# Two SwiGLU input projections of a streaming-encoder layer computed as 2x2 block products, seven in place of eight, with GpSimd forming the sums of weight blocks

## The chip, the core and the metric

The kernel runs on one core of one Trainium2 chip. The engines named below are PE (TensorE, matrix products), PEld (TensorE loading its stationary operand), ACT (ScalarE), DVE (VectorE), POOL (GpSimd) and SP (SyncE, which here only issues transfers). The metric is the device time of one execution in microseconds (us); lower is better.

## The reference

One layer of a hybrid encoder on 512 prompt tokens and 64 sample tokens, model width 1024, feed-forward width 4096, all in float32. What the change touches is the SwiGLU block, which stands at the start and at the end of the layer:

```python
def swiglu(x, w_in, w_out):
    a, b = jnp.split(x @ w_in, 2, axis=-1)      # w_in 1024 x 8192
    return (jax.nn.silu(a) * b) @ w_out         # w_out 4096 x 1024

x = x + 0.5 * swiglu(rmsnorm(x, norm_ffn1), w_ffn1_in, w_ffn1_out)
x = x + mixer(rmsnorm(x, norm_mix))             # SSD, band attention and mLSTM branches, then w_out
x = x + 0.5 * swiglu(rmsnorm(x, norm_ffn2), w_ffn2_in, w_ffn2_out)
```

A final RMSNorm follows. The mixer's arithmetic is the same in both kernels.

## The kernel before

All 576 tokens run side by side, feature-major: features on the 128 partitions, tokens along the free axis, in two halves of 256 and 320 (`HALVES`). Weights are the stationary operand. Each float32 product is carried by three float32r passes over a high and a low part of both operands (high x high, high x low of the tokens, low of the weights x high), so each tile of 128 input features by 128 output features costs three matmuls for each half of the tokens. One matmul therefore streams 256 or 320 columns, 288 on average.

`weights` (L121) loads the next block of 0.5 MB (`w`, three buffers, issued by SP at L129), casts it to its high part on ACT (`wh`, L132) and subtracts on DVE to get the low part (`wl`, L133). `gemm` (L149) and `matmuls` (L140, the instruction is L146) do the products into one of three PSUM banks (`acc`); with `half_major` a group of blocks is done for one half of the tokens and then for the other. `norm` (L227) writes the token operand, high `XH` on ACT and low `XL` on DVE (`scaled`, L223 and L224, not yet divided by the rms), sums the squares on DVE (`na`, L186) and, through two small PE products (L200, L216), gets `rs`, 1/rms of each token on all partitions.

`ffn` (L308) is the SwiGLU block. `first(i)` makes four tiles of 128 features of the hidden layer: for each one block for a and one for b. The a half is scaled by `rs` on DVE (L322), goes through Silu on ACT (L323) and is scaled again on POOL (L324, `P`); b is multiplied in on DVE (L332, `Q`) and the product is split into `YH` (ACT, L175) and `YL` (DVE, L176). `second(i)` multiplies four such tiles by a row block of w_out: 192 matmuls, 16 evacuations that add to the residual `x` or `R1` (L338). The order is first(0), then first(i), second(i-1) in turn. So one hidden tile of 128 costs 2 blocks x 8 x 3 x 2 = 96 matmuls, and an FFN has 32 of them.

Every instruction goes into its engine's queue in an order that the tile framework's scheduler sets from a simulated timeline; an engine runs its queue in that order, waiting on semaphores. Tiles share buffers by tag, and a tile that reuses a buffer waits until its last reader is done.

```python
def weights(self, desc):                                                    # L121
    w = self.wp.tile([128, 1024], F32, name="w", tag="w", bufs=3)
    nc.sync.dma_start(w, self.I["wblk"][i])                                 # L129
    nc.scalar.copy(hi, w)                                                   # L132
    nc.vector.tensor_tensor(lo, w, hi.bitcast(F32), op=ALU.subtract)        # L133
def matmuls(self, ps, h, hi, lo, c0, step, nk, xh, xl, k0):                 # L140
    for k in range(nk):
        for i, (wt, xx) in enumerate(((hi, xh), (hi, xl), (lo, xh))):
            nc.tensor.matmul(ps[:, :n], wt[:, wsl], xx[:, k0 + k, a:a + n], ...)   # L146
```

Of the kernel before, what the change touches and what calls it, by code (L numbers as in the profile page):

```python
# [15 lines left out]
F32 = mybir.dt.float32  # L16
# [9 lines left out]
NB = 293  # L26
# [3 lines left out]
# the parts of the mixer: attention (pairs of heads), mLSTM (heads), SSD (groups); the recurrences' gates  # L30
# are worked out after number GATES of them
# [4 lines left out]
# columns of the packed per-feature constants  # L36
# [11 lines left out]
# columns of w_in  # L48
# [6 lines left out]
class Hybrid:  # L55
    def __init__(self, ctx, tc, I, O):
        self.tc, self.nc, self.I, self.O = tc, tc.nc, I, O
        self.plan = []
        self.ahead = {}
# [18 lines left out]
    # Slots of a tag are given out in program order, so tiles share a tag only if they are first  # L78
    # written in that order.
# [15 lines left out]
    def setup(self):  # L95
# [13 lines left out]
        # 1 where column >= partition  # L109
# [11 lines left out]
    def weights(self, desc):  # L121
        """The next block of 0.5 MB: its high and low parts."""
# [26 lines left out]
    def gemm(self, tiles, xh, xl, k0=0, half_major=False, order=(0, 1)):  # L149
        """tiles: (desc, [(c0, evac), ...]); desc = (name, row0, rows, col0, cols)."""  # L150
# [27 lines left out]
    def sumsq(self, x, k, h, acc):  # L178
# [5 lines left out]
        sq = self.wp.tile([128, 320], F32, name="sq", tag="sq", bufs=3)  # L184
# [3 lines left out]
    def rsqrt(self, r, src, m, scale):  # L188
        """r[:, :m] = (scale * src + eps) ** -0.5, a few columns."""
# [818 lines left out]
```

## Time and profile before

| what | value |
|---|---|
| time, median of 3 runs | 2066.32 us (2065.57 to 2066.57) |
| span of the profiled execution, first to last instruction | 2064.8 us |
| PE busy | 2046.7 us, 99% |
| DVE / ACT / POOL busy | 1022.9 / 659.1 / 342.5 us |
| weight blocks loaded | 293 of 0.5 MB |
| clock granted to PE, mean | 0.996 |

A profiled execution has no time of its own in the results beside its span; the span lies 1.5 us under the median. Tables of instructions give the line, engine, operation, output and inputs by name, shape, count, busy time, mean duration in ns of one, and the idle time before. A matmul's duration is longer than the distance between two starts, since they are pipelined: the pace is read from starts or from counts in a window.

### The profile page before, as it was taken

How to read it: one execution, taken by the hardware profiler on the slowest of the kernel's cores; microseconds unless marked ns; L12 is line 12 of the kernel's file. 1: busy time of each engine (PE TensorE's matmuls, PEld its weight loads, DVE VectorE, ACT ScalarE, POOL GpSimd, SP SyncE). 2: the span in 40 equal slices, each digit the busy share in tenths (PEclk: the TensorE clock that was granted, in tenths of full speed). 3: DMA queues.
4: the chain of work that ended last, by engine and by line, in shares of the span. 5: the costliest groups of instructions: out<-in, count | busy, mean ns of one | idle time of the engine just before them, and what ended most of it. 6: DMA issues, size and time to landing. Idle time of an engine off the chain costs nothing. (4 is left out here: it accounts for less than half of the span.)

```text
span 2064.8 us, 36478 instructions
## 1 busy us (share of the span) xinstructions
PE 2046.7 (99%) x15269; PEld 1999.4 (97%) x15269; DVE 1022.9 (50%) x1956; ACT 659.1 (32%) x1174; POOL 342.5 (17%) x448
## 2 busy tenths in 40 slices
PE   8999999999999999999999999999999999999998
PEld 7999999999999888989999999999999999999998
DVE  6344444444446856466777535345444444444445
ACT  3222222222224345454445223234322222222223
POOL 4101101101100010202443201320111011011011
PEclk9999999999999999999999999999999999999999
DMA  3222222222224322322333222222222222222221
GB/s 140 85 86 85 84 83 82 82 82 83 82 93 150 109 87 70 101 65 72 114 104 105 70 82 108 103 81 82 82 82 83 83 86 85 85 83 82 82 82 57
DMA packets 63131, 182.90 MB, mean 89 GB/s; under 512 B 6752, under 2 KB 18656, under 8 KB 62840
## 3 DMA queue, kind: packets, MB, share of 16 engines
q1 hardware_dynamic: 61992, 179.44, 24.9%
q8 instruction: 120, 1.97, 0.4%
q10 hardware_dynamic: 976, 1.14, 0.2%
q14 instruction: 43, 0.35, 0.1%
HBM read 171.80 MB, written 8.76 MB: 87 GB/s over the span
## 5 line engine op out<-in xcount | busy, mean ns | idle before, releaser
L146 PE MATMUL acc<-XH,wh 128*128 128x256 f32 (+1 forms) x3408 | 1014.3, 298 | 5.1 <-DVE P L322 4.7
L146 PE MATMUL acc<-XL,wh 128*128 128x256 f32 (+1 forms) x3408 | 1012.7, 297 | 2.3 <-DVE XL L224 2.2
L146 PE MATMUL acc<-XH,wl 128*128 128x256 f32 (+1 forms) x3408 | 1014.4, 298 | 0.0
L146 PEld LDWEIGHTS acc<-XL,wh 128*128 128x128 f32 x3408 | 645.2, 189 | 9.3 <-issue 5.4
L146 PEld LDWEIGHTS acc<-XH,wh 128*128 128x128 f32 x3408 | 642.0, 188 | 12.0 <-DVE P L322 5.1
L146 PEld LDWEIGHTS acc<-XH,wl 128*128 128x128 f32 x3408 | 640.9, 188 | 5.1 <-issue 4.7
L132 ACT CAST wh<-w 128x1024 fp32r<-128x1024 f32 x293 | 307.3, 1049 | 829.6 <-PE acc L146 720.0
L133 DVE TENSOR_TENSOR wl<-w,wh 128x1024 fp32r<-128x1024 f32 x293 | 364.9, 1245 | 124.0 <-ACT wh L132 123.3
L146 PE MATMUL acc<-YH,wl 128*128 128x320 f32 (+1 forms) x1280 | 378.6, 296 | 0.0
L146 PE MATMUL acc<-YH,wh 128*128 128x320 f32 (+1 forms) x1280 | 378.4, 296 | 0.0
L146 PE MATMUL acc<-YL,wh 128*128 128x320 f32 (+1 forms) x1280 | 376.9, 294 | 0.0
L324 POOL TENSOR_TENSOR P<-P,rs 128x320 f32<-128x320 f32 (+1 forms) x128 | 145.8, 1140 | 961.8 <-ACT P L323 961.8
L146 PEld LDWEIGHTS acc<-YL,wh 128*128 128x128 f32 x1280 | 241.9, 189 | 0.0
L146 PEld LDWEIGHTS acc<-YH,wh 128*128 128x128 f32 x1280 | 240.4, 188 | 0.2 <-issue 0.2
L146 PEld LDWEIGHTS acc<-YH,wl 128*128 128x128 f32 x1280 | 239.9, 187 | 0.1
L322 DVE TENSOR_TENSOR P<-acc,rs 128x320 f32<-128x320 f32 (+1 forms) x128 | 58.5, 458 | 215.2 <-PE acc L146 212.9
L332 DVE TENSOR_TENSOR Q<-acc,P 128x256 f32<-128x256 f32 (+1 forms) x128 | 58.7, 459 | 184.2 <-PE acc L146 139.1
L338 DVE SCALAR_TENSOR_TENSOR R<-acc,R 128x256 f32<-128x256 f32 (+1 forms) x128 | 58.5, 457 | 84.6 <-PE acc L146 84.3
L323 ACT ACTIVATE P<-P 128x320 f32<-128x320 f32 (+1 forms) x128 | 56.4, 442 | 137.0 <-DVE P L322 137.0
L338 DVE SCALAR_TENSOR_TENSOR x<-acc,x 128x256 f32<-128x256 f32 (+1 forms) x128 | 58.4, 456 | 81.9 <-PE acc L146 81.7
L175 ACT CAST YH<-Q 128x256 fp32r<-128x256 f32 (+1 forms) x128 | 55.1, 430 | 131.5 <-DVE Q L332 131.5
L176 DVE TENSOR_TENSOR YL<-Q,YH 128x256 fp32r<-128x256 f32 (+1 forms) x128 | 58.2, 455 | 30.3 <-ACT YH L175 30.3
(274 smaller groups left out, 1230.9 us busy)
## 6 DMA issues: line engine op xcount, KB each, us to landing
w<-in_wblk SPq DMA_DIRECT2D x293, 512.0 KB, 3.4
b<-scr_rows SPq DMA_DIRECT2D x24, 288.0 KB, 4.2
b<-scr_rows SPq DMA_DIRECT2D x16, 144.0 KB, 3.7
R<-xs SPq DMA_DIRECT2D x1, 2304.0 KB
x<-in_xT SPq DMA_DIRECT2D x2, 640.0 KB, 8.3
xs<-x SPq DMA_DIRECT2D x4, 320.0 KB, 2.9
out_y<-R SPq DMA_DIRECT2D x2, 640.0 KB, 3.2
out_k<-g SPq DMA_DIRECT2D x4, 288.0 KB, 2.3
```

The costliest lines, as they stand in the source:

```text
L132: nc.scalar.copy(hi, w)
L133: nc.vector.tensor_tensor(lo, w, hi.bitcast(F32), op=ALU.subtract)
L146: nc.tensor.matmul(ps[:, :n], wt[:, wsl], xx[:, k0 + k, a:a + n], start=(k == 0 and i == 0), stop=(k == nk - 1 and i == 2))
L175: self.nc.scalar.copy(hi, src)
L176: self.nc.vector.tensor_tensor(lo, src, hi.bitcast(F32), op=ALU.subtract)
L322: nc.vector.tensor_tensor(s[:, :n], ps, rs[:, sl], op=ALU.mult)
L323: nc.scalar.activation(s[:, :n], s[:, :n], AF.Silu)
L324: nc.gpsimd.tensor_tensor(s[:, :n], s[:, :n], rs[:, sl], op=ALU.mult)
L332: nc.vector.tensor_tensor(g[:, :n], ps, box[h][:, :n], op=ALU.mult)
L338: nc.vector.scalar_tensor_tensor(x[:, ot, sl], ps, 0.5, x[:, ot, sl], op0=ALU.mult, op1=ALU.add)
```

## The change

**In the FFN.** Of the 32 hidden tiles the first three (`NPLAIN`) stay as they were. The other 29 of each FFN are done by `swiglu_unit`: the 256 output columns (a tile of b, a tile of a) by 1024 input features are taken as 2x2 blocks of 512 x 128, the tokens as two halves of 288 (`FH`), and the four half results come from seven products of 512 x 128 weights with 288 tokens (`product`, 4 x 3 = 12 matmuls of 288 columns each) in place of eight, in a chain of sums that shares PSUM banks: ACT copies a bank out between two products that accumulate into it (`v`, `u`, `m6`), DVE adds or subtracts banks and copies.

**Token operands.** The seven token operands (`TH`, `TL`, 28 tiles of 288) are made once for each FFN by `operands`, four calls, one for each pair of input tiles: on DVE two scalings by gain and `rs` (L359, 576 columns each), three differences (L363 to L365), and two splits (1440 and 576 columns; ACT for the high, DVE for the low part, L212 and L213). They stand between the fourth, fifth and sixth plain block.

**Weight operands.** `stationary` loads 1 MB (`sblk`) into a `w` buffer, POOL forms four sums of blocks (`sm`, one buffer: one instruction of 1024 columns and two of 512), and ACT and DVE split seven operands of 512 columns in five pieces (512, 512, 1024, 1024, 512).

**Evacuation.** The scaling of Silu's result by `rs` is gone in units (the tokens are already normalised); POOL multiplies one half of each unit (L433, 288 columns).

**Pools.** SBUF and PSUM pools are opened for each phase (FFN, mixer, FFN): in an FFN six `acc` banks in place of three, two `w` buffers of 8 KB a partition in place of three of 4 KB, one `sm`; `norm` of an FFN writes `YH`/`YL`, and the mixer's `XH`/`XL` are tiles of its own phase, in memory that TH and TL had.

```diff
-NB = 293
+NB = 177
+NS = 58
+FH = 288
+NPLAIN = 3
...
+            self.acc = pool("acc", 6, space=bass.MemoryType.PSUM)
+            self.bufs = {"w": 2, "wh": 3, "rs": 1, "P": 6, "Q": 1}
...
+    def operands(self, x, rs, g0, kk):
+        xk = self.wp.tile([128, 4, FH], F32, name="xk", tag="w", bufs=self.bufs["w"])
+        for e in range(2):
+            k = kk + 4 * e
+            nc.vector.scalar_tensor_tensor(xk[:, 2 * e:2 * e + 2, :]..., x[:, k, :],
+                                           self.cst[:, g0 + k:g0 + k + 1], rs, op0=ALU.mult, op1=ALU.mult)
+        d = self.wp.tile([128, 5, FH], F32, name="xd", tag="sm", bufs=1)
+        nc.vector.tensor_tensor(d[:, 0:2, :], xk[:, 0:2, :], pair(3), op=ALU.subtract)
+        nc.vector.tensor_tensor(d[:, 2:4, :], xk[:, 1:3, :], pair(0), op=ALU.subtract)
+        nc.vector.tensor_tensor(d[:, 4, :], xk[:, 3, :], xk[:, 2, :], op=ALU.subtract)
+        for sl, src in ((slice(0, 5), d), (slice(5, 7), xk[:, 0:4:3, :])):
+            self.split(src, self.TH[:, sl, kk, :], self.TL[:, sl, kk, :])
+    def stationary(self, desc):
+        w = self.wp.tile([128, 4, 512], F32, name="w", tag="w", bufs=self.bufs["w"])
+        nc.sync.dma_start(w, self.I["sblk"][i]...)
+        s = self.wp.tile([128, 4, 512], F32, name="sm", tag="sm", bufs=1)
+        nc.gpsimd.tensor_tensor(s[:, 0:2, :], w[:, 0:2, :], w[:, 1:3, :], op=ALU.add)
+        nc.gpsimd.tensor_tensor(s[:, 2, :], s[:, 0, :], w[:, 2, :], op=ALU.add)
+        nc.gpsimd.tensor_tensor(s[:, 3, :], s[:, 2, :], w[:, 3, :], op=ALU.add)
+        for names, src in (((self.T_X1,), s[:, 0, :]), ((self.T_A11,), w[:, 0, :]),
+                           ((self.T_X3, self.T_X4), s[:, 2:4, :]), ((self.T_A22, self.T_A21), w[:, 2:4, :]),
+                           ((self.T_X2,), s[:, 1, :])):
+            tag, bufs = ("wh", "wl") if n == 2 else ("vh", "vl"), self.bufs["wh"]
...
+            self.split(src, *parts)
+    def swiglu_unit(self, desc, slot):
+        self.product(pa, ops, self.T_X1, True)
+        nc.scalar.copy(v, pa)
+        self.product(pb, ops, self.T_A11, True)
+        nc.vector.tensor_tensor(g[:, 1, :], pb, v, op=ALU.add)
+        self.product(pa, ops, self.T_X3, False)
+        nc.scalar.copy(u, pa)
+        self.product(pc, ops, self.T_X4, True)
+        nc.scalar.copy(m6, pc)
+        self.product(pa, ops, self.T_A22, False)
+        nc.vector.tensor_tensor(s0, m6, pa, op=ALU.subtract)
+        nc.scalar.activation(s0, s0, AF.Silu)
+        self.product(pc, ops, self.T_A21, False)
+        nc.vector.tensor_tensor(s1, pc, u, op=ALU.subtract)
+        nc.scalar.activation(s1, s1, AF.Silu)
+        nc.gpsimd.tensor_tensor(g[:, 1, :], g[:, 1, :], s1, op=ALU.mult)
+        self.product(pa, ops, self.T_X2, False)
+        nc.vector.tensor_tensor(g[:, 0, :], pa, s0, op=ALU.mult)
+        self.split(g..., self.YH[:, slot, :], self.YL[:, slot, :])
...
-            for j in range(4):
-                tiles.append(((win, 0, 1024, n0, 128), [(0, evac_a(box))]))
-                tiles.append(((win, 0, 1024, 4096 + n0, 128), [(0, evac_b(box, base + j))]))
+                self.gemm(tiles[:3], self.YH, self.YL, half_major=True)
+                for t, kk in zip(tiles[3:], ((0,), (1,), (2, 3))):
+                    for k in kk:
+                        self.operands(x, rs, g0, k)
+                    self.gemm([t], self.YH, self.YL)
+            for j in range(n, 4):
+                self.swiglu_unit((win, 4096 + n0, n0), base + j)
```

The order of the queues at three places, all of DVE. The first is the start of the first FFN, from the weights of the second block on. Before:

```order
L133 TENSOR_TENSOR wl<-w,wh 128x1024
L322 TENSOR_TENSOR P<-acc,rs 128x320 x2
L133 TENSOR_TENSOR wl<-w,wh 128x1024
L332 TENSOR_TENSOR Q<-acc,P 128x320
L176 TENSOR_TENSOR YL<-Q,YH 128x320
L332 TENSOR_TENSOR Q<-acc,P 128x256
L176 TENSOR_TENSOR YL<-Q,YH 128x256
```

There DVE splits blocks and evacuates. With the change the operands of the units are made at this place (`xk` normalised tokens, `xd` their differences, `TL` the low parts); two of the four calls:

```order
L359 SCALAR_TENSOR_TENSOR xk<-R_62,cst,rs 128x576 x2
L213 TENSOR_TENSOR TL<-xd,TH 128x5x288
L213 TENSOR_TENSOR TL<-xk,TH 128x2x288
L363 TENSOR_TENSOR xd<-xk 128x576
L364 TENSOR_TENSOR xd<-xk 128x576
L365 TENSOR_TENSOR xd<-xk 128x288
L170 TENSOR_TENSOR wl<-w,wh 128x1024
L461 TENSOR_TENSOR g<-acc,P 128x256
L359 SCALAR_TENSOR_TENSOR xk<-R_62,cst,rs 128x576 x4
L213 TENSOR_TENSOR TL<-xd,TH 128x5x288
L461 TENSOR_TENSOR g<-acc,P 128x320
L213 TENSOR_TENSOR TL<-xk,TH 128x2x288 x2
```

The split of the next plain block (L170) and the evacuations (L461) now stand between these. The second place is one hidden tile in the middle of an FFN. Before:

```order
L322 TENSOR_TENSOR P<-acc,rs 128x256
L322 TENSOR_TENSOR P<-acc,rs 128x320
L133 TENSOR_TENSOR wl<-w,wh 128x1024
L332 TENSOR_TENSOR Q<-acc,P 128x256
L176 TENSOR_TENSOR YL<-Q,YH 128x256
L332 TENSOR_TENSOR Q<-acc,P 128x320
L133 TENSOR_TENSOR wl<-w,wh 128x1024
L176 TENSOR_TENSOR YL<-Q,YH 128x320
```

And one unit of the change (`vl`, `wl` low parts of its weight operands, out of the sums `sm` or the block `w`):

```order
L417 TENSOR_TENSOR g<-acc,P 128x288
L213 TENSOR_TENSOR vl<-sm,vh 128x512
L213 TENSOR_TENSOR vl<-w,vh 128x512
L213 TENSOR_TENSOR wl<-sm,wh 128x1024
L427 TENSOR_TENSOR P<-P,acc 128x288
L213 TENSOR_TENSOR wl<-w,wh 128x1024
L213 TENSOR_TENSOR vl<-sm,vh 128x512
L431 TENSOR_TENSOR P<-acc,P 128x288
L417 TENSOR_TENSOR g<-acc,P 128x288
L435 TENSOR_TENSOR g<-acc,P 128x288
```

The subtraction that frees the bank `pa` (L427, `s0`) now stands behind a split of a sum. The third place is the end of the first FFN, where the mixer's norm starts. Before:

```order
L224 SCALAR_TENSOR_TENSOR XL<-x,cst,XH 128x256
L186 TENSOR_TENSOR na<-na,sq 128x256
L338 SCALAR_TENSOR_TENSOR x<-acc,x 128x320
L186 TENSOR_TENSOR na<-na,sq 128x320
L224 SCALAR_TENSOR_TENSOR XL<-x,cst,XH 128x320
L338 SCALAR_TENSOR_TENSOR x<-acc,x 128x320
L186 TENSOR_TENSOR na<-na,sq 128x320
L133 TENSOR_TENSOR wl<-w,wh 128x1024
L224 SCALAR_TENSOR_TENSOR XL<-x,cst,XH 128x320
```

With the change:

```order
L466 SCALAR_TENSOR_TENSOR R_62<-acc,R_62 128x256 x6
L466 SCALAR_TENSOR_TENSOR R_62<-acc,R_62 128x320 x6
L540 MEMSET ms 4x1
L541 COPY ms<-cst 4x1
L769 MEMSET r 128x8
L770 MEMSET ss 128x8
L769 MEMSET r 128x8
L770 MEMSET ss 128x8
L261 SCALAR_TENSOR_TENSOR XL<-R_62,cst,XH 128x256 x2
L223 TENSOR_TENSOR na<-na,sq 128x256
L261 SCALAR_TENSOR_TENSOR XL<-R_62,cst,XH 128x256
L223 TENSOR_TENSOR na<-na,sq 128x256
```

Before, the low parts (`XL`) and the sums of squares (`na`) stood between the evacuations of the last tiles; now all of them stand behind the last evacuation (L466), and the splits of the mixer's first three blocks (L170) behind them.

More of the change, by code (lines that the diff above doesn't have):

```diff
@@ L7 @@
-from contextlib import ExitStack, nullcontext
+from contextlib import ExitStack, contextmanager, nullcontext
 import numpy as np
@@ L58, in __init__ @@
         self.plan = []
+        self.splan = []
         self.ahead = {}
@@ L293, in norm_out @@
                     self.rsqrt(r, pt[:, :2], 2, 1.0 / 1024)
-        tr = [self.ps(tag) for tag in "ssvx"]
+        tr = [self.acc.tile([128, 512], F32, name="acc", tag="acc") for _ in range(4)]
         for k in range(8):
@@ new lines, in product @@
+    def product(self, ps, ops, t, start):
+        hi, lo = ops[t]
+        for kk in range(4):
+            wsl = slice(kk * 128, (kk + 1) * 128)
+            for i, (wt, xx) in enumerate(((hi, self.TH), (hi, self.TL), (lo, self.TH))):
+                self.nc.tensor.matmul(ps, wt[:, wsl], xx[:, t, kk, :], start=(start and kk == 0 and i == 0),
+                                      stop=(kk == 3 and i == 2), skip_group_check=True)
+    def swiglu_unit(self, desc, slot):
+        nc = self.nc
+        ops = self.stationary(desc)
+        bank = lambda: self.acc.tile([128, 512], F32, name="acc", tag="acc")[:, :FH]
+        e = lambda: self.P((128, FH))
+        g = self.wp.tile([128, 2, FH], F32, name="g", tag="g", bufs=3)
+        pa = bank()
+        self.product(pa, ops, self.T_X1, True)
+        v = e()
+        nc.scalar.copy(v, pa)
+        pb = bank()
+        self.product(pb, ops, self.T_A11, True)
+        nc.vector.tensor_tensor(g[:, 1, :], pb, v, op=ALU.add)
+        self.product(pa, ops, self.T_X3, False)
+        u = e()
+        nc.scalar.copy(u, pa)
+        pc = bank()
+        self.product(pc, ops, self.T_X4, True)
+        m6 = e()
+        nc.scalar.copy(m6, pc)
+        self.product(pa, ops, self.T_A22, False)
+        s0 = e()
+        nc.vector.tensor_tensor(s0, m6, pa, op=ALU.subtract)
+        nc.scalar.activation(s0, s0, AF.Silu)
+        self.product(pc, ops, self.T_A21, False)
+        s1 = e()
+        nc.vector.tensor_tensor(s1, pc, u, op=ALU.subtract)
[3 more added lines that the diff above has]
+        nc.vector.tensor_tensor(g[:, 0, :], pa, s0, op=ALU.mult)
+        self.split(g.rearrange("p h t -> p (h t)"), self.YH[:, slot, :], self.YL[:, slot, :])
@@ L318, in evac_a, with ffn @@
+    def ffn(self, x, rs, g0, win, wout, last=(0, 1)):
+        nc = self.nc
+        self.TH = self.xt.tile([128, 7, 4, FH], F32R, name="TH", tag="TH", bufs=1)
+        self.TL = self.xt.tile([128, 7, 4, FH], F32R, name="TL", tag="TL", bufs=1)
         def evac_a(box):
@@ L877, in run @@
         nc, tc = self.nc, self.tc
[L878 to L898 removed]
+        x = self.R1
@@ new lines, in run @@
+        with self.ffn_phase("a"):
+            self.setup()
+            with tc.tile_pool(name="a0", bufs=1) as pool:
+                xin = self.I["xT"].rearrange("(k p) t -> p k t", p=128)
+                first = [("w_ffn1_in", 0, 1024, c, 128) for c in (0, 4096, 128)]
+                for k in range(0, 8, 2):
+                    eng = nc.sync if k % 4 else nc.scalar
+                    eng.dma_start(x[:, k:k + 2, 0:256], xin[:, k:k + 2, 0:256])
+                    if k == 0:
+                        self.ahead[first[0]] = self.weights(first[0])
+                        nc.scalar.dma_start(self.cst, self.I["cst"])
+                for d in first[1:]:
+                    self.ahead[d] = self.weights(d)
+                for k in range(0, 8, 4):
+                    nc.sync.dma_start(x[:, k:k + 4, 256:576], xin[:, k:k + 4, 256:576])
+                rs = self.norm_first(x, C_G1, self.YH, self.YL, first[2], pool)
+            with tc.tile_pool(name="axt", bufs=1, reuse_waits="tile") as self.xt:
+                self.ffn(x, rs, C_G1, "w_ffn1_in", "w_ffn1_out")
+                for a, n in HALVES:
+                    for k in range(0, 8, 2):
+                        nc.sync.dma_start(self.xs[:, k:k + 2, a:a + n], x[:, k:k + 2, a:a + n])
@@ L955, in pack @@
     out["wblk"] = wb
+    sb = np.empty((NS, 128, 4, 4, 128), f32)
+    for i, (n, c1, c2) in enumerate(splan):
+        for q, (c, r) in enumerate(((c1, 0), (c1, 512), (c2, 512), (c2, 0))):
+            sb[i, :, q] = w[n][r:r + 512, c:c + 128].reshape(4, 128, 128).transpose(1, 0, 2)
+    out["sblk"] = sb.reshape(NS, 128, 2048)
     cst = np.zeros((128, C_N), f32)
```

135 lines of the change are left out of this document (76 added, 59 removed).

## The prediction

> **What bounds the kernel now.** I read the page first: its busy line, and the chain of work that ended last. The shares say how much of the span each engine worked; the chain, what the end hung on.
>
> ```profile
> span 2064.8 us, 36478 instructions
> PE 2046.7 (99%) x15269; PEld 1999.4 (97%) x15269; DVE 1022.9 (50%) x1956; ACT 659.1 (32%) x1174; POOL 342.5 (17%) x448
> PE 45%; ACT 1%; DMA 0%; POOL 0%; issue 0%; DVE 0%; POOLq 0%; DVEq 0%; SPq 0%
> ```
>
> PE is busy throughout, and no other engine has a share to speak of in the chain. Since a busy PE is not PE at its peak, I looked next at the pace: a window of the first FFN with the matmuls of L146 alone (columns: length, PE busy and count, PEld, clock, DMA share, GB/s).
>
> ```profile
> 100.00:600.00 500.00, 500.00 (x3757) 500.00 (x3756) 1.00 0.24 83
> ```
>
> 500 us / 3757 = 133.1 ns a matmul of 288 columns on average, at full clock. That is the unit price. Whether 288 columns cost the mean of 256 and 320 is read from the timeline of PE (start, duration):
>
> ```profile
> 42.02 0.28 PE L146 MATMUL acc<-XH,wl 128*128 128x256 f32 x1
> 44.54 0.28 PE L146 MATMUL acc<-XH,wl 128*128 128x256 f32 x1
> 44.66 0.31 PE L146 MATMUL acc<-XH,wh 128*128 128x320 f32 x1
> 48.03 0.31 PE L146 MATMUL acc<-XH,wl 128*128 128x320 f32 x1
> ```
>
> 21 starts apart, 256 columns take 2.52/21 = 120 ns; 23 apart, 320 take 3.37/23 = 146.5 ns. So 64 columns cost 26.5 ns, a slope and a fixed part, and 288 should cost 133.3. I take 133.1 and keep 146.5 (the wider form's price) as a rival.
>
> The Trainium skill ("TensorE: Matmul & The Clock Gate", Back-to-back issue gap) gives N / 2.4 + 2.5 ns, 122.5 ns for 288; by that the gain worked out next would be 85.3 us in place of 92.6. The rows above are slower than it by 11 ns at both sizes, so the measurement decides.
>
> **The PE term.** Each of 58 units takes 84 matmuls in place of 96: 58 x 12 x 133.1 ns = 92.6 us less. All of it is on the path, since PE is the path.
>
> **Prices of the other engines' work.** Groups by shape in the same window, then one line's durations (min/median/max) and the load:
>
> ```profile
> L133 DVE TENSOR_TENSOR wl<-w,wh 128x1024 fp32r<-128x1024 f32 x79 | 96.8, 1226 | 36.0 <-ACT wh L132 36.0
> L132 ACT CAST wh<-w 128x1024 fp32r<-128x1024 f32 x79 | 82.8, 1049 | 267.7 <-PE acc L146 232.9 <-issue 34.9
> L332 DVE TENSOR_TENSOR Q<-acc,P 128x320 f32<-128x320 f32 x27 | 13.3, 493 | 59.4 <-PE acc L146 59.4
> L332 DVE TENSOR_TENSOR Q<-acc,P 128x256 f32<-128x256 f32 x26 | 11.0, 425 | 19.1 <-POOL P L324 19.1
> L175 ACT CAST YH<-Q 128x256 fp32r<-128x256 f32 x26 | 10.6, 407 | 54.0 <-DVE Q L332 54.0
> L324 POOL TENSOR_TENSOR P<-P,rs 128x320 f32<-128x320 f32 x26 | 40.1, 1543 | 82.3 <-ACT P L323 82.3
> L324 POOL TENSOR_TENSOR P<-P,rs 128x256 f32<-128x256 f32 x26 | 19.2, 740 | 344.1 <-ACT P L323 344.1
> L772 POOL TENSOR_TENSOR b<-b,t x16: 1286/1296/2282, 974.2 to 1131.1; 128x512 f32<-128x512 f32 x16
> w<-in_wblk SPq DMA_DIRECT2D x293, 512.0 KB, 3.4
> out_y<-R SPq DMA_DIRECT2D x2, 640.0 KB, 3.2
> ```
>
> DVE is linear, 425 at 256 and 1226 at 1024: 512 columns 0.69 us, 576 0.76, 1440 1.66, 288 0.46. ACT, 407 and 1049: 512 columns 0.62, 288 0.43. POOL, 740 at 256 and 1296 at 512, 2.17 ns a column: 288 columns 0.81, 1024 2.41. No row has a POOL sum of 1024; its bounds are 2.41 and twice the 512 row's slow end, 4.6, and I take the line's value.
>
> **A unit in steady state.** PE 84 x 133.1 = 11.2 us. POOL 2.41 + 2 x 1.30 + 0.81 = 5.8. DVE: splits 3 x 0.69 + 2 x 1.23 + 0.76, evacuations 4 x 0.46, together 7.1. ACT: splits 3 x 0.62 + 2 x 1.05 + 0.67 and five short operations of 0.43, 6.8. Four units and a `second` (25.6 us of PE) are 70.3 us, in which DVE has 4 x 7.1 + 4 x 1.23 + 16 x 0.46 = 40.7. By sums each engine fits, so units cost PE's time; SP's 1 MB a unit replaces two blocks of 0.5 MB. Each wait within the chain (`v`, `u`, `m6` on ACT, `s0` on DVE) has one product of 12 matmuls, 1.6 us, as cover against 0.43 to 0.46 us of work. If that cover goes, PE waits with all units queued behind.
>
> But POOL and DVE do not run freely side by side. In the timeline:
>
> ```profile
> 55.75 1.23 DVE L133 TENSOR_TENSOR wl<-w,wh 128x1024 fp32r<-128x1024 f32 x1 [0.48 <-ACT wh L132]
> 56.17 1.55 POOL L324 TENSOR_TENSOR P<-P,rs 128x320 f32<-128x320 f32 x1 [3.16 <-ACT P L323]
> 57.71 0.42 DVE L332 TENSOR_TENSOR Q<-acc,P 128x256 f32<-128x256 f32 x1 [0.74 <-POOL P L324]
> ```
>
> POOL's 320 columns should take 0.88 us by its line; started 0.42 us into a DVE subtraction of two SBUF tiles they take 1.55, 0.67 more, where the subtraction still had 0.81 to go. So such operations exclude each other but for 0.14 us at each start. In a unit that is POOL 5.8 + DVE's SBUF splits 5.3 = 11.1 us whole, or 11.1 - 10 x 0.14 = 9.7, of PE's 11.2; the `second` adds slack. I take no wait in steady state.
>
> The Trainium skill ("SBUF — State Buffer", SBUF: two separate sides) calls it an exclusive lock on a shared port pair, held for the whole instruction, for a DVE operation with two SBUF inputs against a GpSimd one. By that a unit has 11.1 of 11.2 us taken, no slack, and 0.14 us more at each of ten hand-overs would bring 12.5 us: 58 x 1.3 = 75 us more than my sum. The row above shows the smaller figure.
>
> **Starts of the phases, where the gain is lost.** Rows of the start, of PE's waits, and of the boundaries (PE busy and count, PEld, DVE, ACT, POOL, clock):
>
> ```profile
> PE acc L146 <- DVE P L322: 4.7, 2, 4.1
> 27.21 0.63 PE L146 MATMUL acc<-XH,wh 128*128 128x320 f32 x1 [4.11 <-DVE P L322]
> 30.26 0.31 PE L146 MATMUL acc<-XH,wl 128*128 128x320 f32 x1
> 28.00:30.00 2.00, 2.00 (x9) 2.00 (x8) 1.79 (x3) 0.00 (x0) 1.97 (x3) 0.50 0.00 0
> 40.67 0.43 ACT L266 COPY rs<-ps_x 128x320 f32<-128x320 f32 x1 [3.09 <-PE ps_x L216]
> 620.00:660.00 40.00, 40.00 (x302) 39.71 (x301) 24.65 (x52) 17.05 (x33) 4.75 (x10) 1.00 0.47 161
> 1425.00:1450.00 25.00, 25.00 (x188) 24.78 (x187) 15.20 (x33) 13.73 (x26) 3.39 (x5) 1.00 0.18 65
> L224 DVE SCALAR_TENSOR_TENSOR XL<-x,cst,XH 128x320 fp32r<-128x320 f32 x8 | 4.4, 546 | 0.5 <-ACT XH L223 0.5
> L224 DVE SCALAR_TENSOR_TENSOR XL<-x,cst,XH 128x256 fp32r<-128x256 f32 x8 | 3.8, 479 | 0.8 <-ACT XH L223 0.8
> L186 DVE TENSOR_TENSOR na<-na,sq 128x256 f32<-128x256 f32 x7 | 2.9, 417 | 0.0
> L186 DVE TENSOR_TENSOR na<-na,sq 128x320 f32<-128x320 f32 x6 | 2.9, 482 | 0.0
> ```
>
> A wait of 4.1 us was followed by half clock: 12 matmuls took 3.05 us where they take 1.76, 1.3 us more. Each wait over some 4 us is charged that.
>
> - Gain at the start: three banks held PE for these 4.1 us until `rs` let them be evacuated; with six it goes on into the second half: -4.1 - 1.3 = -5.4.
> - First FFN, operands. From `rs` at 41.1 DVE has four calls (4 x 0.76 + 0.46 + 1.66 + 0.76 = 5.9 us each, 23.7), three block splits 3.7 and eight evacuations 3.7, 31.1 us; the first unit's 1 MB gets its buffer (that of the last `xk`) 2.9 us before that chain ends. Then the load (bounds 3.4 and 6.8; 640 KB took 3.2, I take 4.5), the first sum 2.4, a cast 0.6: 41.1 + 28.2 + 7.5 = 76.8. PE's three plain blocks end at 41.7 (the first start after the wait for `rs`) + 144 x 0.133 = 60.9. Wait 16; and POOL's scalings (0.74 to 1.54 us each) exclude DVE about four times 0.7, 3 more: 19.
> - First units. The operands of units 1 and 2 have no unit ahead of them to hide behind: between 0 and one unit's 9.7 us of POOL and DVE; half, 5.
> - Mixer boundary: PE busy without a gap before. Now behind the last evacuation (0.49) DVE has 8 x 0.48 + 8 x 0.55 of `XL`, six `na` 2.5 and the first split 1.23, 12.5 us, against six matmuls on hand, 0.8: 11.7. Lower bound 0, if the scheduler's order is kept fed by something I do not see.
> - Second FFN's norm, in PE's queue the sums of squares stand ahead of its first block: evacuation 0.5, six `na` 2.5, one `YL` 0.55, two `na` 1.0, then the first split 1.2 and an `na` 0.5, less two products: 6.
> - Second FFN's operands: the same chain from `rs`, which comes some 10 us after its first block starts: 10 + 28.2 + 7.5 + 3 = 48.7 against six blocks of PE, 38.3: 10; its first units 5: together 15.
> - Five waits over 4 us (two, one, one, one): 6.5.
>
> Sum: -92.6 - 5.4 + 19 + 5 + 11.7 + 6 + 15 + 6.5 = -34.8: a span of 2030, and with the median's 1.5 us more 2031.5. Removed at no price: the rest of the Silu scaling on POOL and the smaller evacuations, all beside PE. The mixer's queues keep their shape; I charge nothing, PE's gaps there being under 2 us.
>
> **Rivals.**
> Lock-bound units (the other sign): `s0` on DVE stands right behind a split of a sum; that split can wait for a POOL sum of 2.41 us, and 2.41 + 1.23 + 0.46 - 1.6 of cover is a wait of 2.5 us a unit, 145 us at most. POOL works 52% of a unit, so 72 likely: 2104. A unit saves 1.6 us and the starts cost 1.0 of it back; from 0.6 us of wait a unit the change loses. For: 9.7 of 11.2 taken. Against: the banks and six `P` let the queue of the next unit's products fill waits.
> The starts are hidden: the boundary and second FFN's waits vanish as in before's gapless rows; only 19 + 5 stay: about 2000. Against: the queues are in order, and the order shows the chains.
> 288 columns cost 320's 146.5 ns: a unit takes 12.3 us against 12.8, 58 x 0.47 = 27 us saved, 2097. Against: two sizes on one line.
>
> **Numbers.** Forecast 0.74 (2008 to 2060 for itself: the starts' total halved or with 25 us more), lock-bound 0.12, hidden starts 0.08, width 0.04, no change in sum 0.02. Two kernels can be told apart from 0.2%, 4 us: faster 0.83 (the forecast's and hidden starts), same 0.03, slower 0.14. The range leaves out the lock-bound case, the width and the hidden starts below 2005.
>
> **What would show it.** Right: in the middle of an FFN PE busy in whole windows with 133 ns a matmul; `sm` sums on POOL near 2.4 and 1.3 us; PE's waits in a handful of long ones at the two FFN starts and the mixer's, clock 0.5 behind them. Wrong: PE waits for `s0`, `u` or `m6` in every unit; sums of 4 us or more; or PE gapless at the mixer's start.

## The result and the profile after

The changed kernel takes 2021.53 us (median of 4 runs, 2020.02 to 2022.94) against 2066.32 before: ratio 0.9782, 95% interval 0.9769 to 0.9796, 44.8 us less. Forecast were 34.8 less, 2031.5, with 2008 to 2060 around it. The page of the changed kernel, its busy line, granted clock by slices and chain:

```profile
span 2021.2 us, 35535 instructions
PE 1968.9 (97%) x14573; PEld 1916.4 (95%) x14573; DVE 1224.0 (61%) x2122; ACT 819.1 (41%) x1474; POOL 594.7 (29%) x564
PEclk8899999999998999999999999999899999999998
PE 93%; DVE 3%; DMA 1%; issue 1%; POOL 1%; ACT 0%; POOLq 0%; SPq 0%; DVEq 0%; ACTq 0%
```

PE is still the path, but 99% have become 97%, and the clock line has dents at the first FFN's start, at the mixer's start, where the second FFN follows the mixer, and at the end. Whether the units themselves run at PE's pace is read from the chain in order of time (start, length, count): three neighbouring pieces of a cycle in the first FFN, then a window of PE in the second (columns as in the prediction).

```profile
212.64 19.05 PE acc L183 x143
231.69 38.30 PE acc L401 x288
282.89 19.05 PE acc L183 x143
1500.00:1900.00 400.00, 400.00 (x3009) 400.00 (x3008) 240.83 (x343) 165.32 (x277) 150.64 (x93) 1.00 0.26 93
```

288 products of L401 in 38.30 us are 133.0 ns each, and a cycle of four units and a `second` takes 282.89 - 212.64 = 70.25 us; the forecast had 133.1 ns and 70.3 us. In 400 us PE has no gap. So the loss lies at the starts and at the end of the kernel; of the starts PE's waits tell (total, times, longest):

```profile
PE acc L183 <- ACT wh L169: 21.2, 5, 5.9
PE acc L183 <- DVE wl L170: 6.2, 5, 2.5
PE ps_x L237 <- DVE na L223: 4.6, 1, 4.6
PE acc L401 <- DVE vl L213: 1.9, 4, 0.6
```

The span by the points at which PE ends its products (read from the timeline of PE, before and after), against the forecast's terms for the same stretch:

| stretch | before | after | difference | forecast |
|---|---|---|---|---|
| start to the first FFN's last product | 637.3 | 608.5 | -28.8 | -25.1 |
| on to a mixer product near 930 us | 311.1 | 324.2 | +13.1 | +13.0 |
| on to the mixer's last product | 486.2 | 482.5 | -3.7 | 0 |
| second FFN, to its last product | 618.8 | 591.7 | -27.1 | -22.7 |
| the tail to the end | 11.4 | 14.3 | +2.9 | 0 |
| sum | 2064.8 | 2021.2 | -43.6 | -34.8 |

What the start of the first FFN looks like, from the timelines of ACT, PE and POOL (start, duration, idle time before and its releaser in brackets):

```profile
36.22 0.42 ACT L303 COPY rs<-ps_x 128x320 f32<-128x320 f32 x1 [8.04 <-PE ps_x L253]
39.71 0.67 ACT L212 CAST TH<-xk 128x576 fp32r<-128x576 f32 x1 [1.64 <-DVE xk L359]
40.29 1.04 ACT L169 CAST wh<-w 128x1024 fp32r<-128x1024 f32 x1
41.38 0.58 PE L183 MATMUL acc<-YH,wh 128*128 128x256 f32 x1 [5.20 <-ACT wh L169]
62.99 1.04 ACT L169 CAST wh<-w 128x1024 fp32r<-128x1024 f32 x1 [1.67 <-DMA w<-in_wblk]
64.09 0.58 PE L183 MATMUL acc<-YH,wh 128*128 128x256 f32 x1 [5.92 <-ACT wh L169]
70.12 2.38 POOL L380 TENSOR_TENSOR sm<-w 128x1024 f32<-128x1024 f32 x1 [6.77 <-DMA w<-in_sblk]
74.66 0.29 PE L401 MATMUL acc<-TH,vh 128*128 128x288 f32 x1
40.00:60.00 20.00, 15.65 (x96) 14.98 (x96) 19.42 (x28) 7.96 (x10) 2.00 (x2) 0.83 0.08 27
```

`rs` is there at 36.6, the first unit starts at 74.7. Between them PE has three plain blocks, 19.2 us, and waits above all twice; in the window from 40 to 60 us DVE is busy 19.42 of 20 us, and PE's clock is at 0.83. The fourth block's cast (L169 at 40.29) stands on ACT behind the cast of the first operands, which waits for `rs`.

At the mixer's boundary, on DVE, ACT and PE:

```profile
608.58 0.49 DVE L466 SCALAR_TENSOR_TENSOR R<-acc,R 128x320 f32<-128x320 f32 x1 [1.27 <-PE acc L183]
609.12 0.46 DVE L261 SCALAR_TENSOR_TENSOR XL<-R,cst,XH 128x256 fp32r<-128x256 f32 x1
612.64 1.03 ACT L169 CAST wh<-w 128x1024 fp32r<-128x1024 f32 x1
613.72 0.58 PE L183 MATMUL acc<-XH,wh 128*128 128x256 f32 x1 [5.18 <-ACT wh L169]
```

The first `XL` follows the last evacuation, as forecast. The tail has a cost that the forecast did not have. Four tiles of the output are scaled out of PSUM and stored, two on ACT and two on DVE; here is DVE's second, before and after the change:

```profile
2059.82 0.74 DVE L302 TENSOR_SCALAR g<-ps_x,sm 128x512 f32<-128x512 f32 x1
2016.76 0.75 DVE L339 TENSOR_SCALAR o<-acc,sm 128x512 f32<-128x512 f32 x1 [2.85 <-DMA out_y<-o]
```

Before, it follows the first at once (these tiles shared a tag of seven buffers, `g`). With the change they share the two `w` buffers, so it waits 2.85 us until the store of the first has landed.

### The profile page after: what moved, and what is told of

Read it like the earlier page. It is cut to its first block, busy times and chain, and to the rows that moved or that the text cites. A ratio compares the mean times of both kernels' runs of the same rounds, so it can differ in the third digit from the quotient of the medians.

```text
span 2021.2 us, 35535 instructions
## 1 busy us (share of the span) xinstructions
PE 1968.9 (97%) x14573; PEld 1916.4 (95%) x14573; DVE 1224.0 (61%) x2122; ACT 819.1 (41%) x1474; POOL 594.7 (29%) x564
## 3 DMA queue, kind: packets, MB, share of 16 engines
q10 hardware_dynamic: 976, 1.14, 0.2%
## 4 chain that ended last, share of the span: by engine, by line
PE 93%; DVE 3%; DMA 1%; issue 1%; POOL 1%; ACT 0%; POOLq 0%; SPq 0%; DVEq 0%; ACTq 0%
PE acc L183 55%; PE acc L401 31%; PE ps_s L652 1%; PE ps_v L663 1%; PE ps_x L640 1%; DMA w<-in_wblk 1%; PE ps_s L919 1%; PE ps_v L939 0%; DVE YL L261 0%; PE ps_x L945 0%; DVE YL L213 0%; PE ps_x L610 0%; DVE vl L213 0%; DVE TL L213 0%; DVE sq L297 0%
## 5 line engine op out<-in xcount | busy, mean ns | idle before, releaser
L183 PE MATMUL acc<-YH,wh 128*128 128x256 f32 (+1 forms) x1472 | 440.3, 300 | 14.4 <-ACT wh L169 14.4
L183 PE MATMUL acc<-YL,wh 128*128 128x256 f32 (+1 forms) x1472 | 440.2, 299 | 2.8 <-DVE YL L261 2.5
L183 PE MATMUL acc<-YH,wl 128*128 128x256 f32 (+1 forms) x1472 | 438.0, 300 | 3.7 <-DVE wl L170 3.7
L183 PE MATMUL acc<-XH,wh 128*128 128x256 f32 (+1 forms) x1360 | 407.9, 300 | 6.8 <-ACT wh L169 6.8
L183 PE MATMUL acc<-XH,wl 128*128 128x256 f32 (+1 forms) x1360 | 407.5, 300 | 2.5 <-DVE wl L170 2.5
L183 PE MATMUL acc<-XL,wh 128*128 128x256 f32 (+1 forms) x1360 | 408.8, 301 | 0.0
L169 ACT CAST wh<-w 128x1024 fp32r<-128x1024 f32 x177 | 185.6, 1048 | 292.3 <-PE acc L183 225.5
L401 PE MATMUL acc<-TH,wh 128*128 128x288 f32 x928 | 274.2, 296 | 0.0
L401 PE MATMUL acc<-TL,wh 128*128 128x288 f32 x928 | 273.5, 295 | 0.0
L401 PE MATMUL acc<-TH,wl 128*128 128x288 f32 x928 | 271.6, 295 | 1.9 <-DVE wl L213 1.9
L183 PEld LDWEIGHTS acc<-XH,wh 128*128 128x128 f32 x1360 | 257.3, 189 | 13.7 <-ACT wh L169 7.4
L183 PEld LDWEIGHTS acc<-XH,wl 128*128 128x128 f32 x1360 | 257.1, 189 | 7.8 <-issue 4.7
L183 PEld LDWEIGHTS acc<-XL,wh 128*128 128x128 f32 x1360 | 257.4, 189 | 5.9 <-issue 5.4
L170 DVE TENSOR_TENSOR wl<-w,wh 128x1024 fp32r<-128x1024 f32 x177 | 224.5, 1269 | 61.2 <-ACT wh L169 61.2
L380 POOL TENSOR_TENSOR sm<-w 128x1024 f32<-128x1024 f32 x58 | 141.0, 2432 | 327.0 <-DVE vl L213 136.3
L401 PE MATMUL acc<-TH,vh 128*128 128x288 f32 x696 | 206.1, 296 | 1.7 <-ACT vh L212 1.7
L401 PE MATMUL acc<-TH,vl 128*128 128x288 f32 x696 | 205.3, 296 | 1.9 <-DVE vl L213 1.9
L401 PE MATMUL acc<-TL,vh 128*128 128x288 f32 x696 | 205.7, 296 | 0.0
L466 DVE SCALAR_TENSOR_TENSOR R<-acc,R 128x256 f32<-128x256 f32 (+1 forms) x256 | 115.1, 454 | 117.4 <-PE acc L183 116.2
```

What stands on the lines that cost most here:

```text
L380: nc.gpsimd.tensor_tensor(s[:, 0:2, :], w[:, 0:2, :], w[:, 1:3, :], op=ALU.add)
L401: self.nc.tensor.matmul(ps, wt[:, wsl], xx[:, t, kk, :], start=(start and kk == 0 and i == 0), stop=(kk == 3 and i == 2), skip_group_check ...
L466: nc.vector.scalar_tensor_tensor(x[:, ot, sl], ps, 0.5, x[:, ot, sl], op0=ALU.mult, op1=ALU.add)
```

## The experiments

All but one start from the changed kernel (2021.5 us); times are medians. The kernel before took 2066.3 to 2067.5 us when it was timed beside them, so differences of about 1 us between runs say nothing.

### What the change costs without the units

```diff
-            n = NPLAIN if i == 0 else 0
+            n = 4          # every hidden tile plain; no operands, no stationary
+        self.XH = c.tile([128, 8, T], F32R, name="XH")   # XL too: kept for the whole kernel
...
```

> All 32 hidden tiles of both FFNs stay plain, 96 matmuls each, under the changed kernel's pools by phase, six banks and two w buffers; the token operands XH and XL are kept for the whole kernel. It prices the rest of the change without the units. Theory A (the seven products pay in full, 58 x 12 x 133.1 ns = 92.6 us, and part of what was given back belongs to the phases and not to the units): before 2066.3, less 5.4 at the start, plus the waits at the two boundaries (9 and 6 us in the changed kernel, without the operands) and 2.9 us at the tail, 2079, range 2070 to 2085. Theory B (the phases cost nothing by themselves, what was given back is the price of the units' operands): 2061 to 2066.

Measured 2077.29, ratio to before 1.0049 (1.0032 to 1.0066): theory A. Everything but the units costs 11 us; the units with their operands give 55.8 of the 92.6 that their missing products are worth. The longest waits left are those of the boundaries, 5.00 us at the mixer and 4.85 at the second FFN. The mixer's is smaller than the changed kernel's 9.3 in all; `XH` and `XL` lie outside the phases here, and the run below that moves them alone has 4.3.

### One of the suspects of the start: the buffer of `xk`

```diff
-        xk = self.wp.tile([128, 4, FH], F32, name="xk", tag="w", bufs=self.bufs["w"])
+        xk = self.wp.tile([128, 4, FH], F32, name="xk", tag="xk", bufs=1)
```

> The scratch xk of the token operands gets a buffer of its own, so that no weight load waits for it. Theory A (the first units wait for DVE's chain of operands, 24 us from rs on; the late loads of the sixth block and of the first unit lie beside it): 0 to 4 us less than 2021.5. Theory B (the waits of 5.9 us at 64 us and 3.3 us at 1461 us, with their cold clock, are the loads' that stood behind xk): 2004 to 2010.

Measured 2014.42, between the two. The waits of PE, and POOL's first sum:

```profile
PE acc L401 <- ACT vh L212: 22.2, 2, 16.5
67.69 2.34 POOL L380 TENSOR_TENSOR sm<-w 128x1024 f32<-128x1024 f32 x1 [14.89 <-DVE TL L213]
```

The block loads are early now, the three plain blocks run without a break, and what was two long waits with their cold clock is one wait of 16.5 us: the unit's first sum waits for the buffer that it shares with `xd`, that is for DVE's last operand. So the loads behind `xk` were 4 us of the chain (the units start at 70.7 in place of 74.7), and the second FFN is 3.3 shorter (588.4 in place of 591.7); the rest is DVE's chain. Theory A has the larger part of the mechanism, but its range was too narrow by 3 us.

### More cover for the chain

```diff
-NPLAIN = 3
+NPLAIN = 4
-                for t, kk in zip(tiles[3:], ((0,), (1,), (2, 3))):
+                for t, kk in zip(tiles[3:], ((0,), (1,), (2,), (3,), ())):
-        g = self.wp.tile([128, 2, FH], F32, name="g", tag="g", bufs=3)
+        g = self.wp.tile([128, 2, FH], F32, name="g", tag="g", bufs=4)
```

> Four plain tiles at the start of each FFN in place of three (56 units in place of 58), the four calls of operands between the five plain blocks that follow; a fourth buffer for g. Theory A (PE waits there because its plain blocks end before DVE's chain of operands does): the two more blocks cover 12.8 us of PE in each FFN, less 4.3 us that they add to DVE and 1.6 us that the lost unit would have saved, 7 us each, and fewer cold stretches: 2008, range 2004 to 2012. Theory B (the waits belong to each operands call, its buffers and loads, whatever stands around it): two units less cost 3.2 us, 2022 to 2026.

Measured 2010.71: theory A. The first FFN's last product ends at 602.3 in place of 608.5, and the second FFN takes 586.6 us in place of 591.7, although PE has two units' saving less. What was missing there was cover. (The fourth buffer for `g`, which the fourth plain tile needs, was not tried alone.)

### The same wait from the other end

```diff
+                self.ahead[tiles[3][0]] = self.weights(tiles[3][0])
                 for t, kk in zip(tiles[3:], ...
```

> The kernel with the three edits together (1993.06 us) and one more: the fourth plain block is loaded, cast and split ahead of the first operands. In that kernel PE waits 5.2 us for this cast at 40 us, since it stands in ACT's queue behind the first operands' cast, which waits for rs. Theory A (DVE's chain from rs on sets when the units can start, so that a wait removed ahead of it comes back as one): within 3 us of 1993, the gain that of a cold stretch less. Theory B (that wait is a loss of its own): 1985 to 1988.

This run starts from the kernel with three edits together that closes this part (1993.06 us). Measured 1994.25: theory A; against the kernel before, timed beside each, both have the ratio 0.9645. The wait moved, from the fourth block to the fifth (PE, first without the edit, then with it):

```profile
40.45 0.58 PE L185 MATMUL acc<-YH,wh 128*128 128x256 f32 x1 [5.20 <-ACT wh L171]
50.37 0.58 PE L185 MATMUL acc<-YH,wh 128*128 128x256 f32 x1 [8.09 <-ACT wh L171]
```

### Three banks

```diff
-            self.acc = pool("acc", 6, space=bass.MemoryType.PSUM)
+            self.acc = pool("acc", 3, space=bass.MemoryType.PSUM)
```

> The changed kernel with three accumulation banks in the FFNs in place of six. Theory A (six banks are what lets a unit's products start while the last unit's banks still wait for evacuation): the start's wait of 4 us comes back with its cold clock, 5.4, and each of 58 units loses the queueing of its neighbour, up to 0.46 us (one DVE evacuation) each, 27 us: 2027 to 2054, 2040 taken. Theory B (banks matter only at the start): 2027.

Measured 2032.43, 10.9 more. The wait at the start is back, the first unit starts 3.7 us later (78.4), and a cycle takes 236.09 - 165.47 = 70.62 in place of 70.25 us:

```profile
PE acc L183 <- DVE P L449: 4.1, 1, 4.1
165.47 40.00 PE acc L401 x300
236.09 40.00 PE acc L401 x300
```

The time lies in theory A's range, but its mechanism is far smaller than I had put it: six cycles of 0.37 us are 2 us in an FFN and not 13. By PE's products the first FFN ends 6.0 later and the second takes 2.9 more; theory B, the start alone, falls too.

### POOL against DVE

In the middle of the first FFN (150 to 560 us), the sum of 1024 columns on POOL (min/median/max), and DVE's splits by shape, which take 690 and 1220 ns alone (the rows' means mix those that stood beside a sum with those that did not):

```profile
L380 POOL TENSOR_TENSOR sm<-w x23: 2388/2402/2405, 154.6 to 534.1; 128x1024 f32<-128x1024 f32 x23
L213 DVE TENSOR_TENSOR vl<-sm,vh 128x512 fp32r<-128x512 f32 x48 | 42.7, 890 | 1.9 <-ACT vh L212 1.2
L213 DVE TENSOR_TENSOR wl<-w,wh 128x1024 fp32r<-128x1024 f32 x24 | 35.3, 1472 | 25.6 <-ACT wh L212 25.3
```

This sum never waits; DVE's splits are longer by what overlaps. Matched one by one over this window, the seventeen splits of 512 columns that started while POOL's second sum (L381) ran were 547 ns longer, with 687 ns of the sum still to go, six beside its third (L382) 1085 at 1223, and six of 1024 columns beside L380 992 at 1129: each time what was left of the sum, less 0.14 us. An extra addition on POOL in each unit, first on data of its own:

```diff
         nc.gpsimd.tensor_tensor(s[:, 3, :], s[:, 2, :], w[:, 3, :], op=ALU.add)
+        nc.gpsimd.tensor_tensor(self.Z, self.Z, self.Z, op=ALU.add)
```

> Each unit gets one more POOL addition of 1024 columns on a scratch tile of its own that nothing reads, 2.4 us behind the third sum. Theory A (POOL and DVE operations with SBUF inputs alone exclude each other, and the units have little room): POOL still has 60% idle, but the DVE splits that stand against the addition are late by up to 2.4 us each and PE has at most one product of cover; between 30 and 140 us more than the changed kernel's 2021.5, 2080 taken. Theory B (they run side by side; POOL is busy 29% of the span and 58 x 2.4 = 140 us more fit into its idle time): 2021 to 2026.

Measured 2091.30, 69.8 more, but not where I had put it. Since nothing ties these additions to a unit, the scheduler let them run together at the start of each FFN:

```profile
L384 POOL TENSOR_TENSOR Z<-Z x58: 1885/2342/3188, 33.7 to 1572.3; 128x1024 f32<-128x1024 f32 x58
60.00:160.00 100.00, 73.23 (x455) 69.49 (x456) 83.29 (x73) 37.27 (x60) 81.18 (x40) 0.83 0.17 64
160.00:560.00 400.00, 399.44 (x3000) 398.98 (x2999) 243.33 (x342) 160.60 (x267) 152.91 (x92) 1.00 0.27 94
```

POOL is busy 81% there, and PE 73%. The time is not theory B's: 140 us of POOL work that PE does not need cost 70 us. DVE's splits of 512 columns out of sums take 1832 ns in the mean there (690 alone), so exclusion has a part in it; but the extra additions also stand in POOL's own queue between the units' sums, and this run does not part the two. It says nothing on the middle of the FFN either, so a second form was made, which reads the sums:

```diff
+        nc.gpsimd.tensor_tensor(self.Z, s01, s23, op=ALU.add)      # s01, s23: halves of s
```

> Each unit gets a fourth POOL addition of 1024 columns (2.4 us) behind its three, this time one that reads the sums, so that it must run in its unit; the result goes to a scratch tile that nothing reads. Theory A (POOL and DVE exclude each other, but four units and the second share 70.25 us of PE, of which POOL and DVE's SBUF operations take 4 x 11.1 + 4 x 1.23 = 49.3, so that 4 x 2.4 more fit): only the first units of each FFN, which have no cover, are late, 2.4 us each for three to four of them, twice: 2022 to 2042. Theory B (exclusion binds in each unit by itself, 11.1 of 11.2 us being taken): 54 or more units late by 1.2 to 2.4 us each, 2085 to 2155.

Measured 2040.56, theory A at its upper end. One split in each unit now starts while the extra addition runs: in three units of four it is the first of 1024 columns, which takes 2938 ns there in place of 1220 (2506 in the mean of the row, with the fourth unit's). Yet a cycle takes 70.99 us, 0.74 more:

```profile
L213 DVE TENSOR_TENSOR wl<-sm,wh 128x1024 fp32r<-128x1024 f32 x24 | 60.1, 2506 | 10.9 <-ACT wh L212 10.9
216.68 19.05 PE acc L183 x143
287.67 19.05 PE acc L183 x143
```

Six such cycles in an FFN are 4.4 us, and the first five units, up to the first whole `second`, take 4.4 us more (73.6 to 145.4 us; 74.7 to 142.1 without the addition). So exclusion is real, and a unit's own 11.2 us are not its limit: the `second` and the queue of operands absorb 2.4 us a unit almost whole. With one SBUF operand in place of two:

```diff
+        nc.gpsimd.tensor_scalar(self.Z, s01, 0.5, None, op0=ALU.mult)
```

> As the run with the fourth addition, but the extra POOL operation is a multiplication of the first two sums by a constant, which reads one SBUF operand (1024 columns) in place of two. Theory A (what excludes DVE is any POOL operation on SBUF): the same time as that run within 3 us, if the operation is as long. Theory B (only two-operand additions exclude it): less, 2021 to 2026, and DVE's operations of 512 and 1024 columns beside it keep 0.69 and 1.23 us.

Measured 2035.30, between the theories: 5.3 less than the two-operand form although the operation takes 3.21 us (median) and not 2.57. The cycle is 70.33. What excludes what here is read from the timelines of POOL and DVE:

```profile
224.33 3.21 POOL L383 TENSOR_SCALAR Z<-sm 128x1024 f32<-128x1024 f32 x1
225.23 1.12 DVE L213 TENSOR_TENSOR vl<-w,vh 128x512 fp32r<-128x512 f32 x1
226.28 0.68 DVE L213 TENSOR_TENSOR vl<-sm,vh 128x512 fp32r<-128x512 f32 x1
```

The multiplication takes 2.77 us in the 12 units in which no split runs as it starts, and 3.21 to 3.29 in the 46 in which one does. Of the splits of 512 columns, the 21 that start 0.5 to 0.9 us behind its start end 2.0 to 2.1 us behind it (1117 to 1522 ns in place of 690). The 41 that start 1.9 to 2.3 us behind it take 674 to 694 ns, as alone, though the multiplication still runs for 0.5 to 1.3 us. So a POOL operation with one operand in SBUF excludes DVE too, but only in its first part, and each theory has half of it. Last, the sums left out:

```diff
-        nc.gpsimd.tensor_tensor(s[:, 0:2, :], w[:, 0:2, :], w[:, 1:3, :], op=ALU.add)    # and two more
+        s = w
```

> The three POOL sums of each unit are left out: the operands that were sums are split from the loaded block itself, so the output isn't the layer's. Theory A (in the middle of an FFN the sums stand beside PE's work at no price, they cost only where a unit has none ahead of it): 2.4 + 0.7 us at each of the first two or three units and cold clock, 2005 to 2018. Theory B (the sums and what they exclude hold the units back throughout): 58 x 0.5 us or more, below 1992.

Measured 2009.15: theory A. The same splits take 710 and 1225 ns, the cycle 224.56 - 154.37 = 70.19, 0.06 less. What is saved, 7.4 us of the first FFN, lies at its start: the first unit 1.8 us earlier, and the first five 5.0 us shorter (62.3 in place of 67.3). The second FFN is 5.9 shorter, its first five units 4.5 of that (62.3 in place of 66.8).

```profile
L213 DVE TENSOR_TENSOR wl<-w,wh 128x1024 fp32r<-128x1024 f32 x47 | 57.6, 1225 | 37.9 <-ACT wh L212 37.8
L213 DVE TENSOR_TENSOR vl<-w,vh 128x512 fp32r<-128x512 f32 x69 | 48.1, 710 | 18.2 <-ACT vh L212 17.8
154.37 38.24 PE acc L398 x288
224.56 38.24 PE acc L398 x288
```

### The boundaries: where the norms' tiles lie

```diff
-            self.XH = self.fp.tile([128, 8, T], F32R, name="XH", tag="XH", bufs=1)
+            xp = pool("xp", 1)           # opened behind the phase's other pools
+            self.XH = xp.tile([128, 8, T], F32R, name="XH", tag="XH", bufs=1)     # XL too
```

> The mixer's XH and XL get a pool that is opened behind the phase's other pools, so that they lie over TH and TL alone, which are free 45 us before the first FFN ends, and not over its weight buffers. Theory A (the boundary's 9 us come from the norm standing behind the last evacuation because its tiles lie in memory that is in use until then): 2012 to 2018, 2015 taken. Theory B (they come from the first loads of the mixer, which stand in SP's queue behind the stores of the residual, which wait for the last evacuation): 2020 to 2023.

Measured 2017.52: theory A, at the weak end. `XL` now stands between the evacuations, as it did before the change, and PE's waits at the boundary fell from 9.3 to 4.3 us:

```profile
605.46 0.55 DVE L262 SCALAR_TENSOR_TENSOR XL<-R,cst,XH 128x320 fp32r<-128x320 f32 x1 [0.63 <-ACT XH L261]
606.10 0.49 DVE L467 SCALAR_TENSOR_TENSOR R<-acc,R 128x320 f32<-128x320 f32 x1
608.40 0.40 DVE L224 TENSOR_TENSOR na<-na,sq 128x256 f32<-128x256 f32 x1
```

The sums of squares (`na`) still stand behind the last evacuation. They were moved alone:

```diff
-                acc = self.wp.tile([128, 320], F32, name="na", tag="na", bufs=2)
+                acc = self.np.tile([128, 320], F32, name="na", tag="na", bufs=2)   # np: a pool for the whole kernel; sq too
```

> The two scratch tiles of the norms' sums of squares (na, sq) lie in a pool that lives for the whole kernel, no longer in the phase's pool. Theory A (the wait of 4.6 us for the second FFN's norm, and its cold clock, come from the phase change: the sums can't start before the mixer's last buffers are free): 2012 to 2018, 2015 taken. Theory B (the sums are late since they follow the last evacuation in DVE's queue anyway): 2019 to 2023.

Measured 2010.50, beyond theory A. At the second FFN the sums now stand between the mixer's last evacuations (L1006), from 1395 us on, where they began at 1415.67; so `rs` comes earlier, and DVE's chain of operands with it. From the mixer's last product to the first unit it takes 48.2 us (1410.3 to 1458.5) in place of 56.6: 8.4 less, of which the first units give back 2.5 (the second FFN as a whole takes 585.8 in place of 591.7). Another 4.0 are saved at the mixer's start.

```profile
1397.94 0.42 DVE L224 TENSOR_TENSOR na<-na,sq 128x256 f32<-128x256 f32 x1
1399.36 0.42 DVE L1006 TENSOR_TENSOR R<-acc,R 128x256 f32<-128x256 f32 x1 [1.00 <-PE acc L184]
```

### All three together

Four plain tiles, `XH`/`XL` behind the other pools, `na`/`sq` for the whole kernel; P with five buffers.

> The three edits of this group together (four plain tiles, XH and XL behind the other pools, na and sq for the whole kernel; P with five buffers). If each takes away a wait of its own place they add up: 7 to 14 us at the FFN starts, 6 at the mixer's, 6 at the second norm: 1999, range 1994 to 2006. If they are names of one and the same wait, no better than the best alone: 2008 to 2015.

Measured 1993.06 (1992.16 to 1994.01), ratio to before 0.9645 (0.9632 to 0.9658): 28.5 us below the changed kernel, more than 10.8 + 4.0 + 11.0 of the three alone, and 0.9 below the lower end of the range. So the three are not names of one wait. It beats both kernels.

```profile
PE 1956.3 (98%) x14597; PEld 1906.9 (96%) x14597; DVE 1215.0 (61%) x2116; ACT 813.3 (41%) x1462; POOL 592.2 (30%) x560
PEclk8999999999999999999999999999999999999999
```

At 50 us a digit the dents in the clock are gone but for the start's; by the trace stretches of half clock of 3.4 and 6.8 us are left at the mixer's start (606 us) and the second FFN's (1401 us). This also speaks on theory B of the boundary. In SP's queue the mixer's loads still stand behind the last store of the residual (`xs`):

```profile
601.90 0.38 SPq L1037 DMA_DIRECT2D xs<-R  x1
602.38 0.91 SPq L168 DMA_DIRECT2D w<-in_wblk  x2
```

PE's waits at that place are down to 2.7 us nevertheless, none of them for a weight.

## Why the prediction was right, and where its terms were off

The path was right: the missing products pay in full, the units run without a wait, and the starts give half of it back. Some of the terms agree better than their makeup.

- **The PE term** (92.6 us) came in whole: 133.0 ns a product, 70.25 us a cycle, no gap. The rival with the price of 320 columns is out. The formula of the Trainium skill ("TensorE: Matmul & The Clock Gate", Back-to-back issue gap) was no fair rival beside it: it gives 122.5 ns, but that section of the Trainium skill means it for an isolated matmul and says that it counts wrongly in a stream of weight loads and matmuls.
- **Steady state without a wait** is right, and so is its reason: POOL and DVE exclude each other but for 0.14 us, and the `second` adds slack. The run with 2.4 us more on POOL in each unit lost 0.19 us a unit. The lock-bound rival is out. The Trainium skill's exclusive lock ("SBUF — State Buffer", SBUF: two separate sides) is borne out by the splits that grow with their overlap, less 0.14 us each. The 75 us that I worked out from a lock held whole did not come: with still more on POOL, units borrowed room from their `second`. The run with one operand differs from that section of the Trainium skill, which has the lock held for the whole instruction: there DVE was held only in the first part.
- **The start's gain** was put at 5.4. The third block's second half ends at 35.4 where it ended at 39.8, 4.4; three banks cost the first unit 3.7.
- **The chain of operands** in the first FFN: 28.2 + 7.5 + 3 from `rs` on, 38.7 us; measured 38.0, of which PE's blocks cover 19.2. The term of 19 is right, and its path too: the first unit's load goes out 28.4 us after `rs`. Its first low part (`vl`) and PE's last plain block both end at 74.82, so PE shows no wait there.
- **The cold clock was counted twice there.** In those 19 us PE waits 13.0 (5.20 + 1.14 + 5.92 + 0.78) and loses the other 6 by running slowly. In the chain of work that ended last no piece of PE stands between 36.2 and 85.1 us, only DVE, ACT, POOL and transfers; so PE's slow work there cost nothing. The 2.6 us that I charged to this FFN's two waits on top were no cost of their own: up to the first unit the change loses 13.7 us against before (74.7, where the three plain tiles had ended at 61.0), and I had -5.4 + 19 + 2.6 = 16.2.
- **Second FFN, up to its first unit**: 16.2 us lost (56.6 after the mixer's last product in place of 40.4); I had 6 + 10 + 2.6 = 18.6. The 6 and 10 alone give it. But here PE is in the chain from 1421 to 1458, so the half clock behind the norm's wait (1420 to 1427) did cost, and the 6 and the 10 must hold an error the other way; in which of them, the runs do not say.
- **First units**, 5 us as a half between two bounds: without the sums the first five units of the two FFNs are 5.0 and 4.5 us shorter. By the rows, from the first unit to the FFN's last product, 3.8 and 3.0 of the 46.3 are lost against before. The half was a guess, and that it came so near is luck.
- **The mixer's boundary**: 11.7 + 1.3 forecast, 13.1 measured, but made up otherwise. PE waits 9.3 us in three pieces, not 11.7 in one, and loses most of the rest at half clock, which lasted 13.7 us (611 to 625) and not for 12 matmuls. The chain was `XL` and six `na` behind the last evacuation; moved singly, the first gave 5.4 of it and the second 4.0, all three edits together 9.9. The 3.7 us won later in the mixer I had not looked for, and their cause was not tried.
- **The tail**: 2.9 us that I had at none. It is the second pair of output tiles, which waits 2.7 and 2.85 us for a buffer of `w` until a store has landed; that term is a price of the pools by phase, which leave two such buffers. It was not tried with more.

The errors that cancel (the tail against the mixer) hide in the sum. Those that remain, 3.7 us in the first FFN (2.5 before its first unit, 1.2 behind) and 4.4 in the second (2.4 and 2.0), all have one direction, and the span came out 9 us better than forecast.

## What to carry to other kernels

Fewer products on the engine that bounds pay by their count in the steady stretches; what they cost is paid where a phase starts, so look there for the chain that must end before the first cheap product can run, and for the plain work that can cover it: one plain tile more in each FFN was worth 11 us here in all. A pool by phase can be a barrier: here tiles that lay over buffers in use until the last evacuation pulled a norm behind it, and small scratch tiles that live through the phases took part of that away. It also leaves fewer buffers to what comes last, as the tail shows. And a wait that is removed ahead of a chain comes back behind it (5.2 us became 8.1): price the chain and not the waits.

## What the runs showed of the hardware

I had expected exclusion from one row. What the runs add is how regular it is: beside POOL additions of 512 and 1024 columns a split that starts second grew by what was left of the addition, less 0.14 us, and the operation that starts second takes the delay (POOL's sum of 1024 columns stayed within 2388 to 2405 ns, a split that started in the extra addition took 2938 ns in place of 1220). With one SBUF operand in place of two, POOL held DVE up only in its first part: splits that started 1.9 us or more behind its start kept their 674 to 694 ns while it ran on. Not expected either was that PE's half clock can be free: after the first FFN's waits of 5.2 and 5.9 us it ran at 0.5 for 6.8 and 10.2 us, and neither shows in the chain that ended last. Nor did it take a wait of 4 us, as I had charged it: one of 3.26 us, up to 1461 us, was followed by 6.8 us at 0.5.
